# A hybrid encoder layer on one core: both parts of an operand in one product of 512 columns

## The chip, the core and the metric

The kernel runs on one core of a Trainium2 chip. The engines are named as in the profile: PE is TensorE (matrix products), DVE is VectorE, ACT is ScalarE, POOL is GpSimd, SP is SyncE, which issues the loads of the weights. The metric is the time of one execution on the device in microseconds; the kernel before has a median of 1154.0 us over three runs.

## The reference, cut to what matters

One layer works on 528 tokens (16 meta tokens and 512 frames) of 1024 features: a feed-forward block, a projection into an RWKV-7 group and a sliding-window attention group, an output projection, a second feed-forward block and a final norm. All is float32.

```python
h = h + 0.5 * swiglu(rmsnorm(h, ffn1_norm), ffn1_w_gate, ffn1_w_up, ffn1_w_down)   # 1024 -> 2816 -> 1024
z = rmsnorm(h, mix_norm) @ w_in                                                    # 20 blocks of 128 columns
y_rwkv = rwkv7_mix(z[..., :RWKV_COLS], ...)      # chunk-wise recurrence, 8 heads of 64
y_attn = ...                                     # chunk-causal window attention
h = h + concat(y_rwkv, y_attn) @ w_out
h = h + 0.5 * swiglu(rmsnorm(h, ffn2_norm), ffn2_w_gate, ffn2_w_up, ffn2_w_down)
return rmsnorm(h, final_norm)[:, N_META:]
```

## The kernel before

**Precision by parts.** Each float32 operand is split into a leading part, rounded to the format that PE reads at its fast rate, and a remainder. A product W x is then three: whi by the leading part of x, whi by its remainder, and wlo by the leading part. ACT makes whi (line 122), DVE subtracts it to get wlo (line 125), once for each unit of weights.

**Units and halves.** The work is cut into units of 128 x 1024 weights. There are 320 of them, because the tokens are handled in two halves: A (the meta tokens and 256 frames, 272 columns) and B (256 columns), each with its own pass over the weights. A unit has 8 blocks along the contraction, so a narrow unit (three products for each block, `mm3` and `mm_part`, which go through `hi_part`, lines 213 and 214) has 24 products with a weight load each. `wide3` takes the first two products of a block as one of 512 columns, since the two parts of x lie side by side: 8 products of 512 columns (line 201) and 8 of 256 (line 203). Its PSUM bank then holds two halves, which must be added: for a gate or up by `both` (an ACT copy, line 207, and a DVE addition, line 208), for a down by a second accumulation on DVE (line 439 beside line 441). Before the change only the second feed-forward block of half B is wide. The meta tokens are dropped in the second block, so that half A has 256 columns there too.

**Order of the steps.** `program` lists the steps by hand: feed-forward 1 of A; four units of feed-forward 1 of B; the input projection of A; the other units of feed-forward 1 of B, beside which A's mixing runs; the output projection of A; the input projection of B; feed-forward 2 of A up to its last ten units, beside which B's mixing runs; the output projection of B; those ten units; feed-forward 2 of B. A feed-forward block goes by three groups of gate and up units, each followed by its down units.

**Mixing beside the units.** `drive` walks the steps and after each unit calls `advance` with that unit's cost, which lets a generator (`tinv`, `chain`, `attention`) emit some of its instructions. A scheduler in the framework then fixes the final order on each engine when the program is built. Once fixed, each engine goes through its own order, so an instruction further back doesn't overtake one that waits. The RWKV part has two stages. `tinv` inverts small triangular matrices by 31 dependent steps on DVE (line 726 multiplies, line 728 reduces), sends the result through DRAM and back, and completes it on PE (lines 753 and 761). `chain` then runs the chunks one after another: products L813 and L816, a copy and an addition (lines 819 and 820), products L828, copies (line 830), products L838 and L846, products L839, L843 and L848, and three operations on the state S (851 twice, 852), after which the next chunk can use S. `group_norm` (product L872) finishes a chunk's output, and the output projection reads it.

**Buffers.** Four PSUM banks serve the units (`bank`), two the chain (`mbank`); whi and wlo have three buffers each, and at most a few units are prepared ahead.

## Time and profile before

| | |
|---|---|
| median of three runs | 1154.0 us (1153.95 to 1160.99) |
| profiled execution | 1158.89 us |
| its span | 1156.7 us |
| granted PE clock, mean over the span | 0.971 of full |
| PE busy | 1114.7 us (96%), 9621 products |
| DVE busy | 826.4 us (71%), 1533 instructions |
| ACT busy | 673.0 us (58%), 1162 instructions |
| weights and other reads of HBM | 173.54 MB |

The profile comes from one execution, 4.9 us above the median; what lies around its span is 2.2 us. A busy PE in this profile is not PE at its peak, since the ends of products are modelled; the distance between the starts of two successive products is the better measure of its pace. Times in the views are microseconds from the start of the span. A granted clock of 1.00 is 2.4 GHz; the lower level is 1.2 GHz, so 0.82 for a stretch means that it was at the lower level for a part of it.

### The profile page before, as it was taken

What the parts mean: (1) busy time and instruction counts of PE and PEld (TensorE: products, weight loads), DVE (VectorE), ACT (ScalarE), POOL (GpSimd) and SP (SyncE); (2) the same over time, 40 slices, a digit from 0 to 9 for tenths busy, and PEclk for the clock granted to TensorE, in tenths of its full rate; (3) what the DMA queues carried; (4) which work ended last, traced back from release to release, by engine and by line L of the source; (5) the groups of instructions that cost most, each with busy time, mean ns of one, the idle gap of its engine ahead of it and who ended that gap; (6) DMA issues with size and microseconds to landing.
All of it is one profiled execution on the core that took longest, in us unless ns stands there. A gap on an engine that the chain in (4) does not pass through costs nothing.

```text
span 1156.7 us, 23838 instructions
## 1 busy us (share of the span) xinstructions
PE 1114.7 (96%) x9621; PEld 1043.9 (90%) x9621; DVE 826.4 (71%) x1533; ACT 673.0 (58%) x1162; POOL 36.4 (3%) x91
## 2 busy tenths in 40 slices
PE   8999999999999998999899999997999899999996
PEld 7999999998999997899899898997889898888885
DVE  7866566776778993356888777995356677777666
ACT  7544444686757645565567685574456366545453
POOL 0000000021000000000002000000000000000000
PEclk8999999999999998899899999998899899999999
DMA  7565655544446554223355445556224356676661
GB/s 270 172 182 185 187 177 179 166 142 151 129 137 182 163 176 131 81 93 112 92 182 167 138 134 169 165 152 163 90 76 122 111 154 216 201 205 194 186 186 66
DMA packets 68721, 178.81 MB, mean 155 GB/s; under 512 B 21620, under 2 KB 26868, under 8 KB 68612
## 3 DMA queue, kind: packets, MB, share of 16 engines
q1 hardware_dynamic: 52384, 173.70, 49.1%
q10 hardware_dynamic: 16228, 3.61, 1.5%
q8 instruction: 75, 1.23, 0.4%
q14 instruction: 34, 0.28, 0.1%
HBM read 173.54 MB, written 3.74 MB: 153 GB/s over the span
## 4 chain that ended last, share of the span: by engine, by line
PE 76%; DVE 13%; DMA 4%; ACT 4%; issue 3%; ACTq 1%; SPq 0%; DVEq 0%
PE big L214 16%; PE big L213 16%; PE big L195 12%; PE big L201 10%; PE big L203 5%; DVE wlo L125 4%; PE big L222 4%; DVE tmp L726 3%; DVE rn L728 2%; PE mx L796 1%; ACT whi L122 1%; PE mx L791 1%; DMA d<-GT 1%; DMA res<-xT_in 1%; DMA d<-rn 1%
## 5 line engine op out<-in xcount | busy, mean ns | idle before, releaser
L122 ACT CAST whi<-raw 128x1024 fp32r<-128x1024 f32 (+1 forms) x321 | 334.8, 1045 | 279.0 <-PE big L214 146.8
L125 DVE TENSOR_TENSOR wlo<-raw,whi 128x1024 fp32r<-128x1024 f32 x320 | 389.7, 1219 | 119.0 <-ACT whi L122 96.2
L214 PE MATMUL big<-h,whi 128*128 128x256 f32 (+1 forms) x528 | 135.2, 289 | 0.0
L213 PE MATMUL big<-h,whi 128*128 128x256 f32 (+1 forms) x528 | 132.0, 288 | 0.0
L213 PE MATMUL big<-n0a,whi 128*128 128x272 f32 (+1 forms) x464 | 123.8, 296 | 8.2 <-ACT n0a L881 3.2
L214 PE MATMUL big<-n0a,whi 128*128 128x272 f32 (+1 forms) x464 | 123.1, 293 | 0.6 <-DVE n0a L342 0.6
L213 PE MATMUL big<-n0b,whi 128*128 128x272 f32 (+1 forms) x464 | 120.3, 290 | 0.4 <-ACT n0b L341 0.3
L214 PE MATMUL big<-n0b,whi 128*128 128x272 f32 (+1 forms) x464 | 119.7, 288 | 0.4 <-DVE n0b L342 0.4
L214 PEld LDWEIGHTS big<-h,whi 128*128 128x128 f32 x528 | 100.6, 191 | 1.5 <-issue 0.9
L213 PEld LDWEIGHTS big<-h,whi 128*128 128x128 f32 x528 | 99.7, 191 | 0.6 <-issue 0.3
L213 PEld LDWEIGHTS big<-n0a,whi 128*128 128x128 f32 x464 | 89.6, 194 | 10.6 <-ACT n0a L881 3.4
L214 PEld LDWEIGHTS big<-n0a,whi 128*128 128x128 f32 x464 | 90.0, 194 | 2.1 <-DVE n0a L342 1.0
L213 PEld LDWEIGHTS big<-n0b,whi 128*128 128x128 f32 x464 | 87.9, 190 | 2.0 <-ACT n0b L341 1.1
L214 PEld LDWEIGHTS big<-n0b,whi 128*128 128x128 f32 x464 | 87.8, 190 | 1.6 <-DVE n0b L342 0.7
L213 PE MATMUL big<-n1a,whi 128*128 128x256 f32 x288 | 76.9, 297 | 8.3 <-ACT n1a L881 4.2
L222 PE MATMUL big<-h,wlo 128*128 128x256 f32 (+1 forms) x528 | 81.3, 289 | 0.0
L195 PE MATMUL big<-n0b,wlo 128*128 128x272 f32 (+1 forms) x464 | 77.4, 288 | 0.0
L195 PE MATMUL big<-n0a,wlo 128*128 128x272 f32 (+1 forms) x464 | 76.4, 286 | 0.0
L214 PE MATMUL big<-n1a,whi 128*128 128x256 f32 x288 | 76.2, 293 | 0.0
L214 PE MATMUL big<-n1b,whi 128*128 128x256 f32 x288 | 76.1, 294 | 0.0
L213 PE MATMUL big<-n1b,whi 128*128 128x256 f32 x288 | 75.7, 292 | 0.0
L222 PEld LDWEIGHTS big<-h,wlo 128*128 128x128 f32 x528 | 71.5, 192 | 1.1 <-issue 0.6
(313 smaller groups left out, 2264.2 us busy)
## 6 DMA issues: line engine op xcount, KB each, us to landing
raw<-w_in SPq DMA_DIRECT2D x319, 512.0 KB, 3.8
outT<-o SPq DMA_DIRECT2D x8, 256.0 KB, 2.6
res<-xT_in SPq DMA_DIRECT2D x2, 544.0 KB, 4.3
res<-xT_in SPq DMA_DIRECT2D x2, 512.0 KB, 9.1
d<-GT ACTq DMA_DIRECT2D x8, 80.0 KB, 3.6
zk<-d ACTq DMA_DIRECT2D x2, 320.0 KB, 4.0
d<-rn ACTq DMA_DIRECT2D x2, 320.0 KB, 3.7
GT<-d ACTq DMA_DIRECT2D x8, 80.0 KB, 4.5
```

The lines of the kernel that those rows point to most:

```text
L122: self.A.copy(out=hi[:, a:a + n], in_=raw[:, a:a + n])
L125: self.V.tensor_tensor(out=lo[:, 0:nk], in0=raw[:, 0:nk], in1=hi[:, 0:nk].bitcast(F32), op=ALU.subtract)
L195: self.PE.matmul(o, lo[:, k], x(k)[:, 0], start=False, stop=(k == ks[-1]))
L201: self.PE.matmul(o, hi[:, i], x(k).rearrange("p a t -> p (a t)"), start=(k == first), stop=False)
L203: self.PE.matmul(o[:, 0:256], lo[:, i], x(k)[:, 0], start=False, stop=(k == last))
L213: self.PE.matmul(o, w, x[:, 0], start=first, stop=False)
L214: self.PE.matmul(o, w, x[:, 1], start=False, stop=False)
L222: self.PE.matmul(o, lo[:, i], x(k)[:, 0], start=False, stop=(k == nk - 1))
L726: V.tensor_tensor(out=m, in0=NT[:n2, 0:k, k].unsqueeze(1).broadcast_to([n2, k, k]), in1=TI[:n2, 0:k, 0:k], op=ALU.mult)
L728: V.tensor_reduce(out=TI[:n2, 0:k, k], in_=m, op=ALU.add, axis=mybir.AxisListType.X)
L791: PE.matmul(b[vr[h], cols(p)], st["vT", p][hs[h], tok:tok + C], self.cent[hs[h], hs[h]], start=True, stop=True)
L796: PE.matmul(b[hs[r], cols(p, 256)], self.BK[p][hs[h], slot, hs[r ^ h]], self.ident[hs[h], hs[h]], start=True, stop=True)
```

## The change

Feed-forward 1 of half B, feed-forward 2 of half A and both output projections become wide. The last up unit of each group is narrow, also in feed-forward 2 of B, which was wide throughout. `wide3` now takes the operand as two runs of 256 columns, since in half A the two parts are not adjacent (the row has 272 columns), and picks the weight block by its number where all 8 are used. The sums of `both` go into two buffers of a pool of their own. In the output projection a second DVE addition takes the second half of the bank.

```diff
@@ -78,6 +78,7 @@
         self.wp = pool("wpl")
         self.tp = pool("tpl")
         self.sl = [pool("slab0")]
+        self.gs = pool("gsum")
         self.big = pool("big", space=PSUM)
         self.mx = pool("mx", space=PSUM)
         self.dr = pool("drm", space=DRAM)
@@ -197,10 +198,11 @@
     def wide3(self, o, w, x, ks, first, last):
 
         hi, lo = w
+        at = lambda i, k: k if len(ks) == NK else i
         for i, k in enumerate(ks):
-            self.PE.matmul(o, hi[:, i], x(k).rearrange("p a t -> p (a t)"), start=(k == first), stop=False)
+            self.PE.matmul(o.rearrange("p (a t) -> p a t", a=2), hi[:, at(i, k)], x(k), start=(k == first), stop=False)
         for i, k in enumerate(ks):
-            self.PE.matmul(o[:, 0:256], lo[:, i], x(k)[:, 0], start=False, stop=(k == last))
+            self.PE.matmul(o[:, 0:256], lo[:, at(i, k)], x(k)[:, 0], start=False, stop=(k == last))
 
     def both(self, o, s):
 
@@ -360,13 +362,14 @@
         W = {hf: TT[hf] - c0[hf] for hf in hfs}
         j0, j1 = GROUPS[f][g]
         st = {}
-        wide = f == 2 and tuple(hfs) == (1,)
+        wide = f == 2 or hfs[0] == 1
 
         def gate(w):
             if wide:
                 b = self.bank()
-                self.wide3(b, w, ns[1], range(NK), 0, NK - 1)
-                st["g"] = {1: self.both(b, self.t(self.fin, [128, 256], "gs", bufs=2))}
+                hf = hfs[0]
+                self.wide3(b, w, ns[hf], range(NK), 0, NK - 1)
+                st["g"] = {hf: self.both(b, self.t(self.gs, [128, 256], "gs", bufs=2))}
                 return
             st["g"] = {hf: self.bank() for hf in hfs}
             self.mm3([st["g"][hf][:, :W[hf]] for hf in hfs], w, [ns[hf] for hf in hfs], NK)
@@ -374,9 +377,10 @@
         def up(j):
             def f_(w):
                 pg, pu = st["g"], {hf: self.bank() for hf in hfs}
-                if wide:
-                    self.wide3(pu[1], w, ns[1], range(NK), 0, NK - 1)
-                    pu = {1: self.both(pu[1], self.t(self.fin, [128, 256], "us", bufs=2))}
+                if wide and j < j1 - 1:
+                    hf = hfs[0]
+                    self.wide3(pu[hf], w, ns[hf], range(NK), 0, NK - 1)
+                    pu = {hf: self.both(pu[hf], self.t(self.gs, [128, 256], "gs", bufs=2))}
                 else:
                     self.mm3([pu[hf][:, :W[hf]] for hf in hfs], w, [ns[hf] for hf in hfs], NK)
                 for hf in hfs:
@@ -409,7 +413,7 @@
         j0, j1 = GROUPS[f][g]
         nk = j1 - j0
         ps = {}
-        wide = f == 2 and tuple(hfs) == (1,)
+        wide = f == 2 or hfs[0] == 1
 
         def down(u):
             def f_(w):
@@ -467,8 +471,9 @@
         def f(d):
             def f_(w):
                 ps = self.bank()
-                self.mm3([ps[:, :256]], w, [lambda k: mo[k // 4][:, k % 4]], 8, WO)
+                self.wide3(ps, w, lambda k: mo[k // 4][:, k % 4], WO, WO[0], WO[-1])
                 r = self.res[hf, d][:, c0:TT[hf]]
+                self.V.tensor_tensor(out=r, in0=ps[:, 256:512], in1=r, op=ALU.add)
                 self.V.tensor_tensor(out=r, in0=ps[:, :256], in1=r, op=ALU.add)
                 self.sq_acc(hf, d, c0)
                 if d == NK - 1:
@@ -1001,9 +1006,6 @@
                 pr.rs1[hf] = pr.rstd(hf, 0, pr.mbank())
             return f
 
-        def fopen():
-            pr.fin = popen("fin")
-
         def mopen():
             pr.mix_init(popen("mix"))
 
@@ -1071,7 +1073,7 @@
         fa = ffn(2, range(len(GROUPS[2])), A, final)
         k = 10
         steps += fa[:-k] + mb[4] + act(lambda: pclose("mix"))
-        steps += pr.w_out(1, mb[5], renorm("f2", 2)) + act(fopen) + fa[-k:]
+        steps += pr.w_out(1, mb[5], renorm("f2", 2)) + act(lambda: popen("fin")) + fa[-k:]
         steps += ffn(2, range(len(GROUPS[2])), B, final)
         pr.rs1 = {}
         pr.consts0()
```

Of 320 units, 142 change from narrow to wide and 3 from wide to narrow, which is 1112 products fewer on PE and 143 instructions more on DVE. The change also moves instructions, since the scheduler sets the order anew. Two places show it.

The first is DVE during A's `tinv` (tmp and rn are its tiles; wlo is the remainder of a unit's weights, res the residual stream, silu and h the feed-forward product, gs the sum of the two halves of a bank). This is the order before, between the 25th and the 26th reduction:

```order
L728 TENSOR_REDUCE rn_3662<-tmp_3665 80x25
L396 TENSOR_TENSOR silu_5797<-big_5771,silu_5797 128x256
L726 TENSOR_TENSOR tmp_3665<-zk_3660,rn_3662 80x676
L125 TENSOR_TENSOR wlo_5767<-raw_5765,whi_5766 128x1024
L398 TENSOR_TENSOR h_855_5796<-silu_5797,h_855_5796 128x256
L728 TENSOR_REDUCE rn_3662<-tmp_3665 80x26
```

The order of the changed kernel between the same two reductions:

```order
L733 TENSOR_REDUCE rn_3645<-tmp_3648 80x25
L445 SCALAR_TENSOR_TENSOR res_153<-big_5834,res_153 128x256
L443 SCALAR_TENSOR_TENSOR res_153<-big_5859,res_153 128x256
L126 TENSOR_TENSOR wlo_5855<-raw_5853,whi_5854 128x1024
L731 TENSOR_TENSOR tmp_3648<-zk_3643,rn_3645 80x676
L445 SCALAR_TENSOR_TENSOR res_153<-big_5859,res_153 128x256
L126 TENSOR_TENSOR wlo_5880<-raw_5878,whi_5879 128x1024
L443 SCALAR_TENSOR_TENSOR res_153<-big_5884,res_153 128x256
L733 TENSOR_REDUCE rn_3645<-tmp_3648 80x26
```

Where one preparation of weights and two feed-forward operations stood between these two steps, there are now two preparations and four accumulations of a down. From the first to the last of the 31 reductions there are 31 preparations where there were 24; in B's `tinv` there are 29 where there were 24. The first product that completes the inverse stands on PE when 143 units have been started, where it was 132 (for B 229, where it was 220).

The second place is PE in A's `chain` (mx are the chain's PSUM tiles, Rs and UV its operands, S the state, big the banks of the units). Before, in the last chunk, between the products on Rs and those that make the new output:

```order
L828 MATMUL mx_5484<-Rs_5445,GT 64x64 x8
L214 MATMUL big_6885<-h_957_6528,whi_6775 128x256
L213 MATMUL big_6885<-h_967_6596,whi_6775 128x256
L214 MATMUL big_6885<-h_967_6596,whi_6775 128x256
L213 MATMUL big_6885<-h_977_6664,whi_6775 128x256
L214 MATMUL big_6885<-h_977_6664,whi_6775 128x256
L222 MATMUL big_6885<-h_907_6188,wlo_6776 128x256
L222 MATMUL big_6885<-h_917_6256,wlo_6776 128x256
L222 MATMUL big_6885<-h_927_6324,wlo_6776 128x256
L222 MATMUL big_6885<-h_937_6392,wlo_6776 128x256
L838 MATMUL mx_5501<-UV_5345,BT_5346 64x64 x8
L846 MATMUL mx_5501<-GT,UV_5345 64x64 x8
```

The changed kernel, from the start of the same chunk (its chain lines are numbered 5 higher) to the products that need UV:

```order
L818 MATMUL mx_5305<-UV_5223,GT 64x64 x8
L821 MATMUL mx_5306<-S,AR_1795 64x64 x2
L821 MATMUL mx_5306<-S,AR_1796 64x64 x2
L821 MATMUL mx_5306<-S,AR_1797 64x64 x2
L821 MATMUL mx_5306<-S,AR_1798 64x64 x2
L877 MATMUL mx_5326<-gsq_5303,bones 128x256
L833 MATMUL mx_5357<-Rs_5323,GT 64x64 x8
L843 MATMUL mx_5374<-UV_5223,BT_5224 64x64 x8
L851 MATMUL mx_5374<-GT,UV_5223 64x64 x8
L844 MATMUL mx_5373<-UV_5223,BT_5224 64x64 x8
```

Nine products of units stood between the two groups of chain products; now none stands between any two of them. In the changed order all 155 units ahead of this point have been started by the third of A's five chunks (the one of the meta tokens counted), and the last two and a half chunks of B have one unit's worth of products beside them.

## Rows read from the trace of the kernel before

**Rows 1.** The page: head, and PE's line (busy us, share, products).

```profile
span 1156.7 us, 23838 instructions
PE 1114.7 (96%) x9621; PEld 1043.9 (90%) x9621; DVE 826.4 (71%) x1533; ACT 673.0 (58%) x1162; POOL 36.4 (3%) x91
```

**Rows 2.** Windows: stretch, length, busy us (instructions) by engine, PE clock, DMA share, GB/s.

```profile
352.00:428.00 76.00, 76.00 (x634) 73.27 (x633) 75.38 (x163) 47.30 (x90) 0.00 (x0) 1.00 0.54 167
428.00:456.00 28.00, 24.75 (x261) 21.43 (x260) 13.58 (x39) 13.33 (x28) 0.00 (x0) 0.82 0.60 163
456.00:566.00 110.00, 108.58 (x1363) 98.34 (x1363) 62.43 (x122) 63.50 (x127) 0.00 (x0) 0.95 0.33 100
722.00:788.00 66.00, 65.29 (x552) 63.02 (x552) 65.53 (x119) 41.11 (x74) 4.42 (x7) 1.00 0.54 162
788.00:829.00 41.00, 34.60 (x341) 29.99 (x341) 14.61 (x41) 19.12 (x43) 2.49 (x4) 0.79 0.39 100
829.00:905.00 76.00, 73.93 (x1042) 67.42 (x1041) 46.05 (x95) 41.40 (x87) 0.00 (x0) 1.00 0.35 107
```

**Rows 3.** Timeline of PE (start, us): narrow, output projection of A, successive units.

```profile
577.25 0.28 PE L213 MATMUL big<-n0b,whi 128*128 128x256 f32 x1
...
580.13 0.28 PE L213 MATMUL big<-n0b,whi 128*128 128x256 f32 x1
```

**Rows 4.** The same: narrow gate and up, then narrow down, feed-forward 2 of A.

```profile
935.90 0.28 PE L213 MATMUL big<-n0a,whi 128*128 128x256 f32 x1
...
938.72 0.28 PE L213 MATMUL big<-n0a,whi 128*128 128x256 f32 x1
...
952.90 0.28 PE L213 MATMUL big<-h,whi 128*128 128x256 f32 x1
...
955.74 0.28 PE L213 MATMUL big<-h,whi 128*128 128x256 f32 x1
```

**Rows 5.** The same: wide units of feed-forward 2 of B, then wide downs.

```profile
1051.25 1.09 PE L201 MATMUL big<-n1a,whi 128*128 128x512 f32 x4
...
1054.04 1.09 PE L201 MATMUL big<-n1a,whi 128*128 128x512 f32 x4
...
1082.02 2.02 PE L201 MATMUL big<-h,whi 128*128 128x512 f32 x8
...
1084.82 2.02 PE L201 MATMUL big<-h,whi 128*128 128x512 f32 x8
```

**Rows 6.** Groups of instructions: count | busy us, mean ns | idle before.

```profile
L125 DVE TENSOR_TENSOR wlo<-raw,whi 128x1024 fp32r<-128x1024 f32 x320 | 389.7, 1219 | 119.0 <-ACT whi L122 96.2 <-PE big L195 13.9 <-ACT Z L756 3.3
L208 DVE TENSOR_TENSOR gs<-big,gs 128x256 f32<-128x256 f32 x22 | 9.2, 417 | 0.0
L207 ACT COPY gs<-big 128x256 f32<-128x256 f32 x22 | 8.0, 366 | 0.0
L439 DVE SCALAR_TENSOR_TENSOR res<-big,res 128x256 f32<-128x256 f32 x24 | 10.0, 420 | 13.6 <-PE big L203 13.3
```

**Rows 7.** Groups of the chain on ACT and DVE.

```profile
L819 ACT COPY Rs<-mx 128x256 f32<-128x256 f32 x8 | 3.0, 371 | 5.1 <-PE mx L813 5.1
L820 DVE TENSOR_TENSOR Rs<-mx,Rs 128x256 f32<-128x256 f32 x8 | 3.4, 422 | 4.7 <-ACT Rs L819 4.7
L851 DVE TENSOR_TENSOR S<-mx,S 128x256 f32<-128x256 f32 x18 | 7.6, 423 | 8.1 <-PE mx L843 6.2 <-PE mx L838 0.8 <-PE mx L839 0.3
L852 DVE TENSOR_TENSOR S<-S,ee 128x256 f32<-128x256 f32 x9 | 3.8, 417 | 0.1
```

**Rows 8.** Windows of the chain's tile mx alone (columns: PE, PEld, DVE, ACT, clock).

```profile
500.00:566.00 66.00, 23.39 (x592) 20.04 (x592) 7.28 (x18) 8.74 (x24) 1.00 0.35 106
```

**Rows 9.** Windows of the tile whi alone, beside the chain and beside tinv.

```profile
500.00:566.00 66.00, 31.82 (x217) 27.60 (x216) 15.87 (x13) 13.60 (x13) 1.00 0.35 106
354.00:428.00 74.00, 51.37 (x373) 46.85 (x372) 28.03 (x24) 24.68 (x24) 1.00 0.54 164
```

**Rows 10.** Waits of PE: line, awaited, total us, times, longest.

```profile
PE big L201 <- DVE res L441: 1.3, 1, 1.3
```

## The prediction, made before the result was known

> **What bounds the kernel now.** I read the page first: PE is busy 1114.7 of 1156.7 us [rows 1], so PE's own pace is the first thing to price. Then the windows by stage: the reader is to see that not all stretches are alike [rows 2]. While tinv runs (352 to 428 and 722 to 788 us), DVE is busy 75.38 of 76 and 65.53 of 66 us, and PE is full as well: two engines are at their limit at once. While the chain runs (456 to 566 and 829 to 905), DVE has room (62.43 of 110, 46.05 of 76) and PE is full of two kinds of work, products of units and small products of the chain. In between lie two stretches in which PE waits for tinv's result to come back, at a granted clock of 0.82 and 0.79. Last I read the timeline of PE for the pace of a unit in either form [rows 3 to 5].
>
> **The pace of PE.** The start-to-start distance of a narrow unit is 580.13 - 577.25 = 2.88 us where the operand's rows have 256 columns [rows 3], 938.72 - 935.90 = 2.82 us where they have 272, and 955.74 - 952.90 = 2.84 us for a down [rows 4]. A wide gate or up takes 1054.04 - 1051.25 = 2.79 us, a wide down 1084.82 - 1082.02 = 2.80 us [rows 5]. So a third fewer products is worth little: the columns are the same, and only the cost around a product goes. 41 gates and ups of feed-forward 1 and 16 output projections save 0.09 us each (5.1 us), 41 gates and ups of feed-forward 2 save 0.03 (1.2 us), 44 downs save 0.04 (1.8 us): **-8.1 us**. A wide product over two separate runs of columns (half A) is in no row; between no saving there and the full 0.03 lie 1.2 us, and I take the full saving, since in rows 4 the longer row costs nothing. The lower end is -6.9.
>
> **The last up of a group.** A narrow last up is not followed by the copy and the addition of its two halves, 0.366 + 0.417 us [rows 6], before the down can start; as a unit it is 0.03 to 0.09 us longer. Of the three places in feed-forward 2 of B, PE stands at one, 1.3 us before L201 [rows 10]. I take 0.78 - 0.09 = **-0.7 us**, between 0 and -1.3.
>
> **DVE during tinv.** The change adds 143 DVE instructions of 0.417 to 0.42 us [rows 6], some 60 us. Most fall where DVE has room and cost nothing: output projections and the chain's stretches are covered by the idle DVE time of rows 2. In tinv there is no room. The order shows that more units are placed there as well: between the first and the last reduction of A stand 7 more preparations (8.5 us), 22 additions of halves (9.2), 8 accumulations (3.4) and three more pairs of feed-forward operations (6 x 0.417 = 2.5): 75.4 + 23.6 = 99 us of DVE. PE has 31 units of 2.79 us there and the attention products of before, about 76 - 24 x 2.87 = 7 us: 93.5 us. So PE comes to wait for wlo and for evictions, some 5.5 us. For B, DVE has 65.5 + 5 x 1.219 + 16 x 0.417 + 9 x 0.42 + 3 x 0.417 = 83.3 us against 29 x 2.79 = 81 us on PE: 2 us. Together **+7.5 us**; nothing if the three buffers of whi and wlo absorb it, 15 us if attention finds its place beside the units. What the 7 and 5 more units themselves cost is no loss: they are missing later.
>
> **The chain without cover.** And that is the main point. Units that have gone into tinv can't be used beside the chain, and the order on PE is fixed. In the order after, A's last three chunks, and about two and a half of B's, have next to no products of units between their steps. Every chunk has steps that PE must wait for: a copy and an addition before the products on Rs (0.371 + 0.422 us) and three operations on S (2 x 0.423 + 0.417) [rows 7], 2.06 us in a row; the copies of UV I leave out, because products of the next chunk stand there. Today products of units fill these waits. 5.5 chunks x 2.06 = 11.3 us. Against that, a product of a unit among chain products costs more: 31.82 / 217 = 147 ns busy against 51.37 / 373 = 138 [rows 9], and by the order 13 units of A and 10 of B, some 550 products of the narrow form, leave the chain: 550 x 9 ns = 5.0 us. Net **+6.3 us**, between -5 (the waits are covered by products of other chunks) and +11.3.
>
> **The clock.** Where the chain runs with products of units between its steps the granted clock is 1.00 (829 to 905) or 0.95; where small products and waits prevail it is 0.82 and 0.79 [rows 2]. A mean of 0.79 means that 42% of the stretch lay at 1.2 GHz. Chain products take 23.39 us for 592 [rows 8], 39.5 ns each, so about 7 us for the 178 of a chunk; 5.5 uncovered chunks are 38 us of PE. At the lower level throughout they would take up to 38 us more; at 42%, the nearest row for a stretch poor in unit products, 16 us more. From this I subtract 5 us for the share of low clock in 456 to 566 (0.95: 11 us at half pace), in which such stretches lie already: **+11 us**, between 0 and +33. The Trainium skill, page "TensorE: Matmul & The Clock Gate", section "Why this matters for your kernels", asks only that TensorE is not left idle for long between bursts. The trace is stricter: in 428 to 456 PE is busy 24.75 of 28 us and the clock is 0.82. By the page's rule the uncovered chunks, with waits of at most some 1.3 us, would keep the full clock, and the sum would lose its +11.
>
> **Sum.** -8.1 - 0.7 + 7.5 + 6.3 + 11 = +16 us. Against the profiled execution (1156.7 us of span, 2.2 around it) that is 1158.9 + 16 = 1174.9; this execution is 4.9 us above the median, so I forecast **1170 us**, slower by 1.4%. A measurement of this kernel can tell about 1% (11.5 us) from no change.
>
> **Rivals.**
> - *The clock holds.* The chunks without cover keep 2.4 GHz, because their small products follow each other closely. For it: no low share at all in 829 to 905, where a third of PE's time is chain work. Against it: 0.82 in 428 to 456 with PE busy. Time: 1154 - 8.1 - 0.7 + 7.5 + 6.3 = 1159, no change that can be told. Chance 0.22.
> - *Faster: the order costs nothing, the pace of PE decides.* The chain has enough products of its own (values of the next chunk, L838 and L846) to fill its waits, DVE's surplus is taken up by the buffers, and units outside the chain run undisturbed: 1154 - 8.1 - 0.7 - 5.0 = 1140. It decides from the point at which a chunk alone takes no longer than its 7 us of products. For it: PE is busy 108.58 of 110 us beside the chain, so that what counts is its work, which shrinks. Against it: the last chunk in the new order has no product between L828 and L838 but must wait for Rs and S. Chance 0.14, with the cases between it and the first rival.
> - *The low clock throughout.* All uncovered chunks run at 1.2 GHz, and DVE's surplus isn't overlapped: 1154 - 8.8 + 15 + 6.3 + 33 = 1199; with either of them halved, 1183 to 1191. For it: in the uncovered chunks no product of 128 x 128 is left, less than in any stretch of rows 2. Chance 0.14.
>
> The forecast itself, the chain uncovered with a part of it at the low clock, has 0.50 and a range of its own of 1161 to 1181.
>
> **How the numbers follow.** The range reaches from between the first two rivals, 1147, to the middle of the last, 1194; it leaves out 0.08 below (half of the faster rival) and a little over 0.1 above. Slower by over 1% (above 1165.5): three quarters of the forecast (0.38), the low clock (0.14) and a rest of the first rival (0.03): 0.55. Faster by over 1% (below 1142.5): 0.09, most of the faster rival. Within 1%: 0.36.
>
> **What would show it.** In the profile after: units of 2.79 us in feed-forward 1 of B and 2 of A where nothing runs beside them (the pace); stretches of tinv 20 us (A) and 15 us (B) longer with DVE full and PE no longer so; in A's last three chunks and B's last two only chain products on PE, with PE empty for about 2 us in each and a granted clock well below 0.95. It would be wrong if the clock stays at 1.00 there, or if a chunk alone takes no longer than 7 us, or if PE stands in tinv for longer than DVE's surplus says, because an eviction in DVE's queue holds a PSUM bank.

## The result, and the profile after

The changed kernel takes 1184.6 us (median of 4 runs, 1182.5 to 1185.6), the kernel before 1154.0 on the same chip: a ratio of 1.025, with an interval of 1.021 to 1.029 (the ratio goes by means, and one of the four runs before took 1161.0). By the medians it is slower by 30.6 us, inside the range and on the side that was forecast, but by nearly twice the sum of 16 us.

The head of the page of the changed kernel, its span and PE's line:

```profile
span 1181.8 us, 21921 instructions
PE 1111.8 (94%) x8509; PEld 983.3 (83%) x8509; DVE 873.6 (74%) x1676; ACT 688.0 (58%) x1236; POOL 35.2 (3%) x91
```

Against [rows 1] PE is busy 2.9 us less and the span is 25.1 us longer. So PE stands empty for 1181.8 - 1111.8 = 70.0 us, where it was 1156.7 - 1114.7 = 42.0. Where the 28 us lie is read from windows. First the changed kernel: the stretch of tinv of half A (from its first to its last reduction), its chain (from there to the first output projection that needs all of it), the same two of half B, and last a piece of A's chain without a unit beside it. Columns: stretch, length, busy us (instructions) by engine, PE clock, DMA share, GB/s.

```profile
364.50:462.00 97.50, 94.60 (x562) 80.91 (x561) 94.09 (x204) 67.71 (x128) 0.00 (x0) 1.00 0.49 162
462.00:584.60 122.60, 101.92 (x1278) 82.82 (x1278) 75.72 (x178) 63.24 (x148) 0.10 (x1) 0.93 0.26 79
723.10:815.10 92.00, 89.22 (x526) 75.26 (x525) 90.76 (x196) 57.73 (x114) 2.17 (x6) 0.98 0.50 160
815.10:936.30 121.20, 102.11 (x1148) 80.79 (x1149) 62.22 (x149) 56.46 (x130) 1.07 (x4) 0.86 0.27 78
541.00:574.00 33.00, 21.81 (x478) 17.97 (x478) 21.71 (x44) 13.08 (x33) 0.00 (x0) 1.00 0.01 2
```

And the kernel before in its own four stretches:

```profile
352.30:426.90 74.60, 74.60 (x623) 71.87 (x622) 73.98 (x159) 47.30 (x90) 0.00 (x0) 1.00 0.55 169
426.90:577.20 150.30, 143.24 (x1680) 129.44 (x1679) 86.33 (x184) 83.61 (x167) 0.10 (x1) 0.91 0.36 107
707.40:784.40 77.00, 74.37 (x616) 71.59 (x615) 75.25 (x159) 50.62 (x94) 3.60 (x6) 0.98 0.53 158
784.40:915.40 131.00, 120.43 (x1460) 109.31 (x1459) 69.31 (x150) 65.82 (x137) 3.31 (x4) 0.91 0.35 102
```

Length less PE's busy time is PE empty. In the chains it goes from 7.1 to 20.7 us (A) and from 10.6 to 19.1 (B), in tinv from 0 to 2.9 and from 2.6 to 2.8: together 20.3 before, 45.5 after. That is 25.2 of the 28 us. tinv is 23 and 15 us longer with both engines full. The chains are shorter, but by less than the units that have left them: 27.7 us in A, where 12 units (at 2.79 us 33 us) are now prepared before its start, and 9.8 us in B, where it is 8 units (22 us).

What PE waited for in A's chain, first before, then after (line, awaited, total us, times, longest):

```profile
PE big L213 <- ACT n0a L881: 3.2, 1, 3.2
PE big L213 <- ACT whi L122: 2.1, 1, 2.1
PE as L930 <- ACT s L929: 1.1, 1, 1.1
PE big L310 <- DVE acc L305: 0.6, 1, 0.6
```

```profile
PE big L203 <- DVE n0a L887: 4.6, 1, 4.6
PE mx L758 <- DMA zk<-d: 3.3, 2, 2.0
PE mx L877 <- ACT gsq L874: 2.4, 1, 2.4
PE mx L818 <- ACT Y L860: 2.3, 3, 0.8
PE mx L796 <- DVE UV L835: 2.2, 2, 1.1
PE mx L844 <- DVE UV L835: 1.1, 1, 1.1
```

The new waits are the chain's own steps: tinv's result coming back through DMA (zk), Y, UV, and the group norm at the end (gsq). The wait for n0a, the operand of the output projection, was there before with 3.2 us. In B's chain the list is shorter: of its 19.1 us the waits for n1a (4.6) and for attention's s (3.7) were there before with 4.2 and 5.0, and new are whi (3.3), gsq (2.4), UV (1.1) and Y (0.8). The timeline of one chunk without units, selected rows of PE, DVE and ACT of the changed kernel (start, us, what, [idle before <- releaser]):

```profile
553.99 0.68 PE L821 MATMUL mx<-S,AR 64*64 64x64 f32 x16 [0.20 <-DVE S L857]
...
555.84 1.75 DVE L880 RECIPROCAL grs<-grs 128x256 f32<-128x256 f32 x1 [0.64 <-ACT grs L879]
...
555.98 0.37 ACT L835 COPY UV<-mx 64x256 f32<-64x256 f32 x1 [0.17 <-PE mx L833]
...
557.63 0.43 DVE L835 COPY UV<-mx 64x256 f32<-64x256 f32 x1
...
558.11 0.62 PE L796 MATMUL mx<-cent,vT 64*64 64x64 f32 x7 [1.10 <-DVE UV L835]
...
562.88 0.68 PE L818 MATMUL mx<-UV,GT 64*64 64x64 f32 x16 [0.81 <-ACT Y L860]
...
563.77 0.68 PE L821 MATMUL mx<-S,AR 64*64 64x64 f32 x16 [0.20 <-DVE S L857]
```

The chunk takes 563.77 - 553.99 = 9.8 us, where the prediction put its products at 7 and its waits at 2.06. One half of the UV copy is on DVE and starts 1.65 us after the half on ACT (557.63 against 555.98), because the previous chunk's reciprocal, 1.75 us, stands ahead of it in DVE's queue.

The pace of a wide unit in half A: first the output projection, whose operand has rows of 256 columns, then feed-forward 2, where the rows have 272 and the two runs of columns lie apart (a gate, and the narrow last up behind it).

```profile
584.59 1.09 PE L203 MATMUL big<-n0b,whi 128*128 128x512 f32 x4
...
587.38 1.09 PE L203 MATMUL big<-n0b,whi 128*128 128x512 f32 x4
```

```profile
960.04 1.08 PE L203 MATMUL big<-n0a,whi 128*128 128x512 f32 x4
...
962.83 0.28 PE L215 MATMUL big<-n0a,whi 128*128 128x256 f32 x1
```

Both distances are 2.79 us, as in [rows 5].

### The profile page after: what moved, and what is told of

Its sections match the earlier page's. It is cut to its first block, busy times and chain, and to the rows that moved or that the text cites. A ratio compares the mean times of both kernels' runs of the same rounds, so it can differ in the third digit from the quotient of the medians.

```text
span 1181.8 us, 21921 instructions
## 1 busy us (share of the span) xinstructions
PE 1111.8 (94%) x8509; PEld 983.3 (83%) x8509; DVE 873.6 (74%) x1676; ACT 688.0 (58%) x1236; POOL 35.2 (3%) x91
## 3 DMA queue, kind: packets, MB, share of 16 engines
q1 hardware_dynamic: 52384, 173.70, 45.5%
## 4 chain that ended last, share of the span: by engine, by line
PE 69%; DVE 17%; ACT 7%; issue 4%; DMA 2%; ACTq 0%; DVEq 0%; SPq 0%
PE big L203 23%; PE big L205 12%; PE big L215 9%; PE big L216 9%; PE big L196 7%; DVE wlo L126 4%; ACT whi L123 2%; DVE tmp L731 2%; PE big L224 2%; DVE rn L733 1%; DVE grs L880 1%; DVE gs L210 1%; DMA d<-tmp 1%; PE mx L801 1%; DVE h L402 1%
## 5 line engine op out<-in xcount | busy, mean ns | idle before, releaser
L123 ACT CAST whi<-raw 128x1024 fp32r<-128x1024 f32 (+1 forms) x321 | 335.0, 1045 | 281.9 <-PE big L203 122.6
L126 DVE TENSOR_TENSOR wlo<-raw,whi 128x1024 fp32r<-128x1024 f32 x320 | 389.3, 1218 | 90.6 <-ACT whi L123 74.5
L203 PE MATMUL big<-h,whi 128*128 128x512 f32 x528 | 141.4, 400 | 6.2 <-DVE h L402 3.1
L203 PEld LDWEIGHTS big<-h,whi 128*128 128x128 f32 x528 | 94.6, 189 | 26.4 <-DVE h L402 4.8
L203 PE MATMUL big<-n1a,whi 128*128 128x512 f32 x360 | 100.2, 399 | 4.6 <-DVE n1a L887 4.6
L203 PE MATMUL big<-n1b,whi 128*128 128x512 f32 x360 | 100.3, 400 | 0.6 <-DVE n1b L956 0.6
L205 PEld LDWEIGHTS big<-h,wlo 128*128 128x128 f32 x528 | 76.5, 193 | 7.8 <-issue 0.9
L203 PEld LDWEIGHTS big<-n1b,whi 128*128 128x128 f32 x360 | 68.2, 192 | 16.0 <-DVE n1b L956 0.7
L205 PE MATMUL big<-h,wlo 128*128 128x256 f32 x528 | 80.7, 287 | 0.0
L215 PE MATMUL big<-n0a,whi 128*128 128x272 f32 (+1 forms) x268 | 72.2, 297 | 4.5 <-ACT n0a L343 2.3
L203 PEld LDWEIGHTS big<-n1a,whi 128*128 128x128 f32 x360 | 62.6, 191 | 14.3 <-DVE n1a L887 5.0
L216 PE MATMUL big<-n0a,whi 128*128 128x272 f32 (+1 forms) x268 | 71.4, 294 | 1.2 <-DVE n0a L344 1.0
L215 PE MATMUL big<-n0b,whi 128*128 128x272 f32 (+1 forms) x268 | 70.9, 294 | 0.4 <-ACT n0b L343 0.3
L216 PE MATMUL big<-n0b,whi 128*128 128x272 f32 (+1 forms) x268 | 70.8, 292 | 0.4 <-DVE n0b L344 0.4
L215 PEld LDWEIGHTS big<-n0a,whi 128*128 128x128 f32 x268 | 51.1, 192 | 6.5 <-ACT n0a L343 2.8
```

What stands on the lines that cost most here:

```text
L123: self.A.copy(out=hi[:, a:a + n], in_=raw[:, a:a + n])
L126: self.V.tensor_tensor(out=lo[:, 0:nk], in0=raw[:, 0:nk], in1=hi[:, 0:nk].bitcast(F32), op=ALU.subtract)
L203: self.PE.matmul(o.rearrange("p (a t) -> p a t", a=2), hi[:, at(i, k)], x(k), start=(k == first), stop=False)
L205: self.PE.matmul(o[:, 0:256], lo[:, at(i, k)], x(k)[:, 0], start=False, stop=(k == last))
L215: self.PE.matmul(o, w, x[:, 0], start=first, stop=False)
L216: self.PE.matmul(o, w, x[:, 1], start=False, stop=False)
```

## The experiments

Two theories stood at first. **Order**: the units that go into tinv are missing beside the chain, and that alone costs. **Added work**: the 143 evictions on DVE, and those on ACT (the copies and additions of the second half of a bank), cost. One table holds all runs: the ratio to the kernel before on the same chip (interval), and from windows like those above the length and, behind the stroke, PE empty in the four stretches.

| kernel | ratio | tinv A | chain A | tinv B | chain B | empty, sum |
|---|---|---|---|---|---|---|
| before | 1 | 74.6 / 0 | 150.3 / 7.1 | 77.0 / 2.6 | 131.0 / 10.6 | 20.3 |
| changed | 1.025 (1.021-1.029) | 97.5 / 2.9 | 122.6 / 20.7 | 92.0 / 2.8 | 121.2 / 19.1 | 45.5 |
| late | 1.009 (1.006-1.012) | 76.5 / 0 | 120.1 / 18.8 | 76.5 / 0.5 | 89.0 / 18.0 | 37.3 |
| noadd | 1.017 (1.014-1.020) | 77.9 / 0.7 | 149.0 / 17.9 | 76.6 / 3.8 | 127.0 / 14.4 | 36.8 |
| uvact | 1.019 (1.016-1.021) | 97.5 / 2.9 | 124.7 / 21.4 | 92.0 / 2.6 | 114.2 / 15.1 | 42.0 |
| held | 1.038 (1.035-1.041) | | | | | |
| pinned | 1.044 (1.041-1.047) | 85.3 / 12.6 | 163.7 / 20.6 | 83.3 / 11.0 | 131.5 / 18.6 | 62.8 |
| pinnoadd | 1.018 (1.016-1.021) | 72.9 / 7.7 | 161.2 / 22.3 | 77.2 / 5.7 | 131.6 / 17.2 | 52.9 |
| f1only | 1.015 (1.013-1.017) | 97.5 / 3.1 | 127.1 / 19.5 | 77.2 / 3.4 | 129.9 / 10.3 | 36.3 |
| f2only | 1.011 (1.008-1.013) | 74.5 / 0 | 145.5 / 7.6 | 92.4 / 2.8 | 122.5 / 19.2 | 29.6 |
| notinv | 1.017 (1.014-1.019) | 77.3 / 0 | 148.0 / 16.8 | 74.6 / 0.9 | 127.5 / 15.8 | 33.5 |
| outside | 1.005 (1.003-1.007) | 75.2 / 0 | 146.5 / 8.1 | 77.7 / 3.1 | 131.3 / 10.8 | 22.0 |
| lateb | 0.995 (0.992-0.997) | 74.0 / 0 | 144.6 / 6.9 | 76.4 / 0.5 | 90.1 / 16.9 | 24.3 |
| latebuv | 0.991 (0.989-0.994) | 74.5 / 0 | 142.7 / 7.0 | 76.4 / 0.5 | 83.7 / 15.8 | 23.3 |

The profiled execution of the kernel before has the longest chain A of the five that have this order there, or nearly (before, f2only, outside, lateb, latebuv: 142.7 to 150.3 us), and is 4.9 us above the median; so the spans of the two profiles differ by 25.1 us, the medians by 30.6.

**held.** Every preparation is tied to a step of tinv that was emitted 14 preparations earlier.

```
- TIW, CHW, ATW = 1.4, 0.55, 0.9
+ TIW, CHW, ATW = 2.0, 0.55, 0.9
+ LAG = 14
...
+ self.seen.append(self.link)              # link: tinv's last column
+ link = self.seen[-1 - LAG] if len(self.seen) > LAG else None
+ if link is not None:
+     self.V.tensor_tensor(out=lo[0:64, 0, 0:1], in0=link, in1=link, op=ALU.subtract)
  self.V.tensor_tensor(out=lo[:, 0:nk], in0=raw[:, 0:nk], in1=hi[:, 0:nk].bitcast(F32), op=ALU.subtract)
```

> Two theories of the 30.6 us between the changed kernel (1184.6) and the one before (1154.0). Theory of the order: the changed order puts 7 (half A) and 5 (half B) more units into tinv, and these are missing later beside the chain, whose last chunks run with nothing to fill their waits. Theory of the added work: the 143 copies and additions of halves themselves hold DVE, ACT and PE. Here all wide products and all added evictions stay; only the order of preparations is held back in tinv, by one tiny DVE operation on a preparation that must wait for a step of tinv, so that 18 and 17 units stand there instead of 31 and 29 and the chain keeps its units. Theory of the order: the chain is covered again, and most of the loss is gone; against that PE idles in tinv, where 18 units of 2.79 us don't fill it: 1160 to 1176. Theory of the added work: 1180 or more.

1199.1 us, slower than the changed kernel, and outside what the theory of the order allowed; the theory of the added work had said 1180 or more. Only its times are used: its profile is of an execution of 5163.9 us, whose cause is not known.

**late.** The kernel before, with tinv's first step put behind a later preparation.

```
+ LATE = 30
...
+ self.lastlo = lo                         # after each preparation
...
+ yield LATE * 2.56                        # in tinv, ahead of the first reduction
+ V.tensor_copy(out=TI[0:n2, 0, 0:1], in_=self.lastlo[0:n2, 0, 0:1].bitcast(F32))
```

> The kernel before, all narrow where it was narrow, with no added eviction; only the order is changed: the planner is made to begin tinv's reductions later among the units, so that as many units stand ahead of its end as in the changed kernel and the chain's last chunks (from X2 on in half A, from Z5 on in half B) run without products of units. Theory of the order: the loss comes although nothing was added, 1175 to 1190. Theory of the added work: 1154, within 6 us.

1164.1 us: between the theories. The rows of its two chains, and the longest waits for chain steps in A's:

```profile
466.50:586.60 120.10, 101.34 (x1348) 90.17 (x1347) 65.01 (x127) 53.14 (x112) 0.10 (x1) 0.87 0.27 78
831.40:920.40 89.00, 71.03 (x1122) 64.75 (x1121) 47.17 (x98) 42.80 (x91) 0.00 (x0) 0.92 0.29 78
```

```profile
PE mx L817 <- ACT Y L859: 3.7, 3, 2.1
PE mx L795 <- DVE UV L834: 2.9, 2, 1.7
PE mx L876 <- ACT gsq L873: 2.4, 1, 2.4
```

PE is empty in them for 18.8 and 18.0 us, nearly as in the changed kernel, without any wide unit or eviction added, and the waits are the same steps, Y, UV and the group norm: units missing beside the chain do empty PE. The total rises less; I put that down to a second way in which the order differs. Attention products in the chains fall from 62 and 68 to 28 and 28; they have gone ahead, among the units. By its trace half A is 9.4 us later at the end of its chain, half B gains 4.4.

**noadd.**

```
- self.A.copy(out=s, in_=o[:, 256:512])
- self.V.tensor_tensor(out=s, in0=o[:, 0:256], in1=s, op=ALU.add)
- return s
+ return o[:, 0:256]
...                                        # and no second accumulation of downs and output projections
```

The kernel leaves out the second half of each wide unit's sum.

> The changed kernel with its wide products, but the second half of each bank is never copied or added (leaves out that part of the sums; the output is not the reference's). DVE and ACT lose the added work; the order, which is planned from DVE's work too, moves about half of the way back: 4 units fewer ahead of tinv's end, the chain uncovered from X3 on in half A and from X7 in half B. Theory of the added work: 1154 - 8 = 1146. Theory of the order: still slower than before, 1160 to 1170, since part of the chain is uncovered.

1172.7 us, above what either theory said. The added work as the only cause falls: without it 19.4 us are still lost.

```profile
442.50:591.50 149.00, 131.15 (x1386) 105.22 (x1385) 80.66 (x181) 77.78 (x171) 0.10 (x1) 0.90 0.29 86
```

tinv has 24 preparations again and is nearly as short as before, but the chain is not covered (17.9 us empty): tinv begins after 110 preparations instead of 105, and 80 attention products are in each chain instead of 62 and 68. The order moves even without the evictions. I put that down to the scheduler's planning, in which a wide unit counts as shorter than a narrow one; no run shows it by itself. A rival is left, that a wide product slows the products beside it; pinnoadd bears on it too, and it is taken up there.

**uvact.** Both copies of UV are on ACT.

```
- (A.copy, V.tensor_copy)[h](out=UV[ur[h], h], in_=X[ur[h], 0:256].rearrange("p (j c) -> p j c", j=4))
+ A.copy(out=UV[ur[h], h], in_=X[ur[h], 0:256].rearrange("p (j c) -> p j c", j=4))
```

> The changed kernel with both copies of UV on ACT, where one of them was on DVE. In the trace of the changed kernel that DVE copy starts only when the previous chunk's reciprocal of the group norm (1.75 us) is over, and PE waits for it (1.10 us before L796 in the chunk at 553.99). If that queue holds the uncovered chain, each uncovered chunk is about 1 us shorter: 1178 to 1181. If the end of a chunk is set elsewhere (the next step waits as long for something else, or ACT is late instead): 1184, within 2 us.

1176.2 us, 22.9 above the kernel before in the same runs, where the changed kernel was 30.6 above: 7.7 us less, more than expected. B's chain is 7.0 us shorter, A's is not. In A the waits for UV (3.3 us) are gone, but PE is empty for 21.4 us, in the changed kernel for 20.7: other steps are now as late.

```profile
PE mx L818 <- ACT Y L860: 3.4, 2, 2.6
PE mx L877 <- ACT gsq L874: 3.2, 1, 3.2
```

In B UV had been 1.1 us of PE's waits; more of the 4.0 us by which PE is empty less there comes from a wait of attention, in the changed kernel and then here:

```profile
PE as L935 <- ACT s L934: 3.7, 2, 1.9
```

```profile
PE as L935 <- ACT s L934: 1.2, 1, 1.2
```

The mean granted clock of the runs is higher as well (0.970 against 0.967), worth 2 to 3 us by the spread in the last section. So the copy does wait in DVE's queue, but that this queue accounts for the gain is not shown.

**pinned.** After held, the sharper form: a table of the kernel before says which reduction of tinv, or which chunk, each preparation stood behind, and ties it there.

```
- TIW, CHW, ATW = 1.4, 0.55, 0.9
+ TIW, CHW, ATW = 1.0, 0.55, 0.9
...
+ half, k = PIN.get(self.np, (0, 0))       # preparation -> half, step of tinv; CPIN: -> chunk
...
+ if x is not None:                        # x: that step's column, or that chunk's mark
+     self.V.tensor_tensor(out=lo[0:64, 0, 0:1], in0=x, in1=x, op=ALU.subtract)
```

> All wide products and all added evictions of the changed kernel, in nearly the order of the kernel before: tiny DVE operations tie the preparations of units to the same steps of tinv and to the same chunks of the chain as before, so that tinv A ends after 127 preparations (before 129, changed kernel 141), tinv B after 216 (218, 226), and the chain keeps units up to its last chunk in half A and up to Z7 in half B. Theory of the order: most of the loss goes; what stays is DVE's surplus in tinv, 24 x 2.06 + 36 = 85 us against 75 in A and about 8 us in B, less the 8 us of the faster pace: 1160 to 1170. Theory of the added evictions: the loss stays wherever the units stand, 1178 or more.

1206.4 us, the slowest of all. Putting the units back with these ties does not bring the time back.

```profile
361.80:447.10 85.30, 72.68 (x390) 58.87 (x391) 79.47 (x209) 48.51 (x103) 0.00 (x0) 0.90 0.41 130
747.10:830.40 83.30, 72.27 (x390) 56.70 (x388) 79.36 (x196) 48.90 (x97) 7.00 (x6) 0.94 0.41 135
```

tinv A takes 85.3 us, close to the 85 that DVE's work had been summed up to, but partly by luck: 22 preparations stand in it instead of 24, DVE is busy for 79.47 us, and 3.3 us of that are the ties themselves. PE is now empty in it for 12.6 us, in tinv B for 11.0. In tinv A the waits are:

```profile
PE big L216 <- ACT whi L126: 6.5, 3, 2.9
PE big L218 <- DVE wlo L139: 3.9, 1, 3.9
PE as L953 <- ACT s L952: 2.3, 1, 2.3
```

PE stands for weights that are not prepared yet. In the changed kernel, with 31 units in tinv A, PE is empty there for 2.9 us only. I read it so that the price is paid either as an empty PE in tinv or as missing cover in the chain, and of these two orders the scheduler's own is the cheaper one; how much the ties add to the other is not separated.

**pinnoadd.** The edits of noadd in the pinned kernel.

> The pinned kernel (wide products in nearly the order of the kernel before) without the copy and addition of the second half of a bank (leaves out that part of the sums; the output is not the reference's). Order and form of the products are those of the pinned kernel, 1206; only the 143 additions and the 70 or so copies are gone. New theory, after the pinned kernel was slower than the changed one: the evictions cost, because DVE is full in tinv and stands in the chain's steps. Then the time falls to that of the kernel before less the faster pace, 1146 to 1152. Rival: a wide product itself is a worse neighbour of the chain's and attention's products than a narrow one, and the tie of the order costs too: 1165 or more. Between 1152 and 1165: both.

1174.9 us. Against the kernel before in the same runs pinned lost 51.3 us and this one 21.8, so at nearly the same order the evictions are worth 29.5 us. tinv falls to:

```profile
360.20:433.10 72.90, 65.24 (x376) 54.02 (x377) 70.96 (x174) 40.98 (x82) 0.00 (x0) 0.95 0.46 145
726.50:803.70 77.20, 71.50 (x411) 58.88 (x410) 72.40 (x166) 41.03 (x74) 6.13 (x4) 0.98 0.45 146
```

12.4 and 6.1 us, 18.5 of the 29.5, come from tinv. But 21.8 us more than before remain, and the ties or a wide product as a neighbour of the small ones may cause them; narrow products with the ties were not run. PE's lines of the pages of noadd (span 1168.1 us) and of this run (1174.1) speak against the neighbour:

```profile
PE 1110.6 (95%) x8509; PEld 981.4 (84%) x8509; DVE 802.3 (69%) x1465; ACT 662.9 (57%) x1119; POOL 35.4 (3%) x91
PE 1101.4 (94%) x8509; PEld 974.8 (83%) x8509; DVE 806.9 (69%) x1547; ACT 663.3 (56%) x1120; POOL 38.3 (3%) x91
```

If wide products made the others longer, PE would be busy for longer than the 1114.7 us of before. It is busy for less, and empty for 57.5 and 72.7 us instead of 42.0. So what these two runs lose is waits, as far as busy time, whose ends are modelled, can tell.

**f1only** and **f2only**: the condition for a wide unit is limited to feed-forward 1 or feed-forward 2, and the output projections are narrow.

```
- wide = f == 2 or hfs[0] == 1
+ wide = hfs[0] == 1                       # f1only; f2only: wide = f == 2
```

> One part of the change alone: wide products in feed-forward 1 of half B, the rest as before. The order is that of the changed kernel around tinv A and that of the kernel before around tinv B. From the two traces, in which the changed kernel had lost 8.6 us when feed-forward 2 began: 1154 + 8 to 10 = 1162 to 1164, if the halves add up. If what stands in half A has consequences later (DMA queues, attention), another number.

> The other part alone: wide products in feed-forward 2 of half A, the rest as before. The order is that of the changed kernel around tinv B. From the two traces: 1154 + 16 to 19 = 1170 to 1173, if the halves add up; with the run that has the part in feed-forward 1 alone they then give the 30.6 us together, less than 2 us for the output projections.

1171.2 and 1167.0 us: 16.1 and 12.0 us above the kernel before in the same runs, 28.1 together, of 30.6. The halves nearly add up, in PE empty too: 16.0 + 9.3 = 25.3 us against 25.2. The split was expected the other way round; half A's share had been read too low from a profile of before with a long chain A.

**notinv.** The changed kernel, but narrow where preparations fall into tinv.

```
- wide = f == 2 or hfs[0] == 1
+ isw = lambda j: f == 2 and tuple(hfs) == (1,) or (F1 or F2) and not (F1 and 6 <= j < 14 or F2 and 6 <= j < 15)
```

F1 stands for `f == 1 and hfs[0] == 1`, F2 for `f == 2 and hfs[0] == 0`; the downs of the group in question are narrow with it.

> The changed kernel, but narrow where the units are prepared while tinv runs (units 6 to 13 of feed-forward 1 of half B and their downs; the last two units and the downs of the first group and units 8 to 14 of feed-forward 2 of half A): about 30 of the 57 gates and ups, 16 of 30 downs. Wide stay the units ahead of tinv, those beside the chain, and the output projections. Theory that the evictions cost only where tinv fills DVE: 1150 to 1160. Theory that they also cost beside the chain, where each of its steps waits in DVE's queue, or by moving units ahead in the order: 1166 to 1176.

1173.1 us. tinv has nearly its old length (77.3 and 74.6 us), and still two thirds of the loss are there: as in noadd, tinv begins 5 (A) and 3 (B) preparations later, and the chains are empty for 16.8 and 15.8 us. That the evictions cost only in tinv falls.

**outside.** Units are wide only far from tinv and the chain.

```
+ outside = lambda j: hfs[0] == 1 and (f == 2 or j < 2) or f == 2 and j >= 20
```

> Wide products only where neither tinv nor the chain's chunks run beside them: the output projections, the first four units of feed-forward 1 of half B, the last ten steps of feed-forward 2 of half A. The order is that of the kernel before. Theory of the order: the pace is gained and nothing is lost, 16 x 0.09 + 4 x 0.09 + 10 x 0.03 = 2.1 us: 1150 to 1152.5. Theory of the added evictions: the 30 additions of 0.42 us cost here too, up to 12 us: 1156 to 1164.

1159.2 us, slower by 4.2 instead of faster by 2.1, in an order that has not moved. One place is seen behind the last output projection of B, on DVE and PE:

```profile
930.44 1.23 DVE L126 TENSOR_TENSOR wlo<-raw,whi 128x1024 fp32r<-128x1024 f32 x1 [0.75 <-ACT whi L123]
...
932.15 0.67 PE L312 MATMUL big<-acc,ones 128*128 128x256 f32 x2 [1.88 <-DVE acc L307]
```

The second accumulation makes the last sum of squares later; it now falls behind a preparation on DVE, and PE waits 1.9 us for it. The same wait stands in the changed kernel. Where the rest of the 4.2 us lies isn't shown.

**lateb** and **latebuv**: late for half B alone; then in addition both UV copies of half B on ACT.

```
+ yield LATE * 2.56 * hf                   # lateb: half B only
...
- (A.copy, V.tensor_copy)[h](out=UV[ur[h], h],
+ (A.copy, A.copy if hf else V.tensor_copy)[h](out=UV[ur[h], h],     # latebuv
...
```

> The kernel before, all narrow where it was narrow, with tinv of half B alone begun later (about 13 units later); tinv A keeps its place. In the run that began both later, half A lost 9.4 us and half B gained 4.4 by the trace, where 40 attention products left the chain for tinv and the stretch before it. If the halves are independent: 1154 - 4 = 1149 to 1151, faster than both kernels. If the gain in half B only made up for a loss in half A (what half A delays is waited for in half B anyway): 1153 to 1158.

> The kernel before with tinv of half B begun later (0.9946 of the time of before, 1148.8 us) and with both copies of UV of half B's chain on ACT. In its trace PE waits 3.3 us for the UV copy that stands on DVE behind a reciprocal, in three of the uncovered chunks of half B. If that wait ends with the copy on ACT: 1145 to 1147. If another step of the chain is then as late (Y or the copies of BT on ACT): 1148 to 1150.

1148.8 and 1144.1 us, both faster than either kernel, if only by 0.5 and 0.9% of the kernel before. B's chain in lateb, then in latebuv:

```profile
817.50:907.60 90.10, 73.18 (x1121) 66.30 (x1120) 47.06 (x98) 43.17 (x91) 0.00 (x0) 0.89 0.27 76
```

```profile
816.20:899.90 83.70, 67.90 (x1122) 61.44 (x1121) 45.40 (x94) 44.30 (x95) 0.00 (x0) 0.96 0.28 81
```

So an uncovered chain need not be a loss: here PE is empty 6.3 us longer in it than before, and the kernel gains. I put that down to the 40 attention products that left the chain for stretches among the units; that it is these alone, no run shows. In both, about half of the gain may be the clock: the runs of lateb have a mean granted clock of 0.974 to 0.984 (0.979 on average, 0.976 for before), those of latebuv 0.981 to 0.985, those of before with it 0.968 to 0.981.

## Why the prediction was right, and where not

- **The size.** 1184.6 lies above the forecast's own 1161 to 1181, where the prediction had put the low clock rival with one of its two terms halved (1183 to 1191). It did not come there by that rival's mechanism, as the points on the chain and the clock show.
- **The pace, -8.1: right.** 2.79 us for a wide unit, in half A too. PE's busy time falls by only 2.9. By the mean granted clocks of the two profiles, 0.971 and 0.967, 2 x 0.029 x 1156.7 = 67 and 2 x 0.033 x 1181.8 = 78 us lie at the lower level of 1.2 GHz, and at half pace 11 us more of it cost up to 5.5, about the difference; that is an estimate.
- **The narrow last up, -0.7: it did not come, because the wait was read wrongly.** The wait of [rows 10] is still there with 1.2 us, where it was 1.3. It lies inside the last downs of feed-forward 2 of B, 12 us after their start at 1126.73, and ends with the accumulation of an earlier down (res), not with the last up's h:

```profile
1138.93 0.70 PE L201 MATMUL big<-h,whi 128*128 128x512 f32 x2 [1.26 <-DVE res L441]
```

```profile
PE big L203 <- DVE res L445: 1.2, 1, 1.2
```

- **DVE in tinv, +7.5: right in its parts, not in what it costs there.** 31 and 29 units, tinv 23 and 15 us longer (20 and 15 forecast), DVE 94.1 and 90.8 us (99 and 83.3 forecast; for B the sum began from a stretch of 66 us, and B's tinv before is 77.0). PE empty grew by 3.1 us only, as the same units fill both engines.
- **The chain without cover, +6.3: the mechanism was right, this is the term that was mis-sized.** PE empty in the two chains grew by 13.6 + 8.5 = 22.1 us. "Rs and S, 2.06 us in a row" was the wrong list: the prediction left the copies of UV out "because products of the next chunk stand there". In the trace PE waits for UV (1.1 us in a chunk), for Y (0.8), for tinv's result (3.3) and, after the last chunk, for the group norm (gsq 2.4; n0a 4.6, where it was 3.2). uvact shows how the list goes on: with UV out of DVE's queue, Y and the group norm are as late in A. The prediction also took the stretches behind tinv for waits for its result: before, PE waits there in A for whi and s (rows above), and in B 5.0 us for s and 1.4 for the result.
- **The clock, +11: right in size at most, and by luck; wrong in place.** In A's uncovered chunks it stayed at 1.00 (541 to 574, with PE busy 21.81 of 33 us), which the prediction had named as a sign that it would be wrong. By the rule of the Trainium skill that the prediction weighed (page "TensorE: Matmul & The Clock Gate", section "Why this matters for your kernels": no long idle gaps between bursts) this was to be expected, and the trace agrees there. It does not agree with 845 to 889 of half B, where PE is busy 42.09 of 44 us, waits at most 1.9 us at a time, and the clock is 0.83. In B's uncovered chunks behind it the clock is low as forecast, 0.88 and 0.85 (889 to 936, rows below). But by length and clock of the rows above, an estimate, 27 and 24 us of the two chains were at the lower level before and 17 and 34 are after: 51 us both times, so that the chains lost nothing by it together. Over all runs the mean clock is 0.965 to 0.968, before mostly 0.974 to 0.979; by the spread of the kernel before (last section) that is some 6 to 8 us, an estimate, and no run shows what lowers it.
- **The sum.** -8.1 + 0 + 3.1 + 22.1 + 2.8 (empty elsewhere, 1.9 of it the wait before L312) + 6 to 8 = 26 to 28 of 30.6 us. The first and the last term are estimates, the others are read from two single profiles.
- **The cause.** late shows that an order without cover empties PE by itself; noadd and notinv, that the order moves, and time is lost, without evictions in tinv; pinned, that putting the units back by ties is worse; pinnoadd, that the evictions are worth 29.5 us in that order. So the loss is neither the order nor the added work alone: evictions lengthen tinv, units are drawn in to fill it (31 preparations in tinv A with them, 24 in noadd and notinv), and the chain lacks them; and the order moves even where no eviction is added. That a wide product slows its neighbours is not seen in PE's busy time, which is no longer in noadd, notinv (1114.5 us) and pinnoadd than before. What stays open is why the scheduler moves the order without evictions, and what the ties cost.

The rows behind the clock of half B, from the changed kernel:

```profile
845.00:889.00 44.00, 42.09 (x457) 33.01 (x455) 20.34 (x56) 27.26 (x65) 0.48 (x2) 0.83 0.25 82
889.00:913.00 24.00, 19.26 (x306) 14.63 (x304) 10.37 (x30) 10.37 (x28) 0.00 (x0) 0.88 0.01 1
913.00:936.30 23.30, 14.14 (x202) 11.99 (x199) 14.20 (x26) 7.17 (x14) 0.00 (x0) 0.85 0.06 16
```

## What to carry to other kernels

Where several engines are filled from one planned order, price a change by what it empties elsewhere: work drawn forward to fill one stretch is cover taken from another, and the latency chain that it covered must be listed step by step, with the queue of every engine that it passes. Before the products of a matmul are merged, compare the unit's time in both forms: here it was 0.03 to 0.09 of 2.8 us, less than one eviction. Where such an order decides, try its start times first: beginning tinv of half B later gained 4.3 us (a part of it with the clock) with nothing added but one small copy that sets the start.

## What the runs showed that I had not expected

- Merging two runs of 256 columns that lie apart into one product costs nothing: 2.79 us for a gate or up in either half.
- The spread between runs of one kernel goes with the clock: the kernel before takes 1149.6 us at a mean granted clock of 0.980 and 1158.0 at 0.970, lateb 1141.6 at 0.984 and 1153.4 at 0.974. A line through all 17 and 12 runs gives 0.7 and 1.1 us for 0.001, and a profile taken at one end shifts every difference that is read from it.
- The clock was 1.00 where PE was busy two thirds of the time with small products (541 to 574), and 0.83 where it was busy 96% with units among them (845 to 889).
